# Weight placement, earlier transposes and two-bank gates in a float32r decoder kernel

## The chip, the cores and the metric

The kernel runs on one core of a Trainium2 chip. The metric is the time of one execution on the device in microseconds (us), the median of several runs. Five engines work side by side: PE (TensorE, the matmuls, with its weight loads shown as PEld), DVE (VectorE), ACT (ScalarE), POOL (GpSimd) and SP (SyncE), which here only issues DMA transfers.

## The reference

Two decoder layers over one sequence of 256 tokens, model width 2048, in float32. Cut to what matters here:

```python
# layer 0: recurrent block, then SwiGLU
y, xb = split(rms_norm(x) @ lru_w_in)            # 2048 -> 2 x 2048
xb = causal_conv4(xb)
r = sigmoid(block_diag(xb, w_rg)); i = sigmoid(block_diag(xb, w_ig))   # 8 blocks of 256
a = exp(-8 * r * softplus(-lam)); u = sqrt(1 - a*a) * (i * xb)
x += (scan(a, u) * gelu(y)) @ lru_w_out
x += (silu(g) * up) @ ffn_w_out   where g, up = split(rms_norm(x) @ ffn_w_in)   # width 5632
# layer 1: one shared K/V, sliding window attention with sinks, then SwiGLU again
k, v = split(rms_norm(x) @ w_kv);  x += attention(rms_norm(x) @ w_q, k, v) @ w_o
x += swiglu(x)
```

## The kernel before

All activations stay in SBUF with features on the partitions and the 256 tokens along the free dimension. A float32 product is made of three float32r matmuls: each operand is cut into a high part and a low part, and high times high, high times low and low times high are summed in PSUM.

**Jobs.** The whole program is a list of jobs, one for each weight chunk of 128 x 1024 floats (two tiles of 128 rows by 512 columns). `stream()` walks the list. At step i it issues the DMA of chunk i + 4 into one of four `raw` tiles, cuts chunk i + 3 into `hi` (copied by ACT, L368) and `lo` (the rest, by DVE, L369), and issues the matmuls of chunk i. Work on activations runs as background tasks, which are stepped between jobs by counters of the DVE and ACT time spent. A scheduler may still move instructions on an engine past each other. A normal chunk has 24 matmuls: 8 weight blocks of 128 x 128, each once against the high half and once against the low half of an activation slot (`a`, `b`), and 8 low weight blocks against the high half (`l`). In `group()` the activations `s` are the loaded weights' counterpart, the moving operand, and `hi`/`lo` are loaded into the array; in `fast_group()` it is the other way round.

**Stages.** Layer 0 begins with `lru()`: groups x0 to x3 and y0 to y3 (8 jobs each) and eight `gates` jobs g0 to g7 in the order `x0 x1 x2 g0 x3 g1 y0 g2 g3 y1 g4 g5 y2 g6 g7 y3`; then `project(lru_out)`. `ffn()` has 22 groups of 8 chunks and then `project(ffn_out)` (4 groups of 22 chunks): groups 0 to 3 are plain (L416), the even groups 4 to 20 are fast groups, the odd ones between are direct groups (L416). A fast group does seven of its eight chunks (`PAIRS`) with seven block products in place of eight, for which `mix()` makes sums of weight blocks in two more slots `mh` and `ml` (DVE and ACT, L380 to L385), and ends in `joined()`, which leaves a result that must be transposed on PE (L785, four transposes; `turn`). These transposes are put in `pend` and done later by `flush()`: in chunk 4 of the next fast group, or in chunk 6 of the last direct group. Layer 1 is `kv()`, `attn()` and again `ffn()`.

**Placement.** From `raw0` on, all tiles are multiples of 256 bytes, but for the 64-byte tile `step`, which stands between slot s6 and slot s7. So the near slots (s0 to s6) stand in phase with `hi` and `lo` (phase 0 of 256 bytes), and the far slots (s7 to s36) at phase 64. Activations stand in far slots. `parts()` sets where in its tile a chunk's `hi` and `lo` begin:

```python
o = 0 if self.jobs[i][2] is not None else self.STEP      # STEP = 32 floats = 128 bytes
```

So a normal chunk's weights stand at phase 128 and those of direct groups, of fast groups and of the queries at phase 0. Of the mixed chunks those in `EVEN` (chunks 0 and 4) put their sums in far slots (phase 64, the phase of the activations), the others in near slots. In the chunks in `EVEN` the products with the sums come first.

**Banks.** PSUM has eight banks of 512 floats. A normal group takes four, a gates job takes four and uses half of each, a fast group takes four. `free_bank` appends to the list of free banks, and `bank()` and `mbank()` take the first of it. `bank4()` takes a whole set of four if all of it is free.

## Time and profile before

| | |
|---|---|
| time before, median of 3 runs | 1972.53 us (1972.23 to 1976.43) |
| profiled execution, its own time | 1969.53 us |
| its span in the profile | 1967.4 us |
| PE busy | 1961.1 us, 16752 matmuls |
| PEld busy | 1933.4 us |
| DVE busy | 1523.4 us |
| ACT busy | 1128.6 us |
| granted TensorE clock | full in every stretch |

The page of the profile gives busy time by engine, the busy share in 40 slices, the chain that ended last, and the costliest groups of instructions with the mean duration of one and the idle time before them. Matmuls overlap: one lasts 277 ns in the records, but the next starts some 113 ns after it. So "PE busy 100%" tells only that PE never stood idle for long; the pace is read from how many matmuls start in a stretch. The windows view counts all instructions that touch a stretch, so its count is one or two above the number of starts. PEld starts are cleaner, since the load of a matmul stands some 0.11 us ahead of it.

### The profile page before, as it was taken

Reading aid. Unit: us, or ns where it says so; the run is one execution under the profiler, and the core shown is the slowest. Engines: PE = TensorE matmul, PEld = TensorE weight load, DVE = VectorE, ACT = ScalarE, POOL = GpSimd, SP = SyncE. Lnnn points to the kernel's source line nnn. Section 1 sums busy time; section 2 is a strip of 40 time slices with the busy share of each in tenths; the row PEclk is TensorE's granted clock in tenths of the full one; section 3 lists DMA queues with packets and bytes.
Section 4 is the critical chain, followed back from the end, with each engine's and each line's share of the span. In section 5 each row is a group of like instructions: output and inputs, shape, how many; then the busy total and the mean of one; then the engine's idle time right before and its main releaser. Section 6 shows DMA issues by size and latency. Waiting matters only on the chain.

```text
span 1967.4 us, 40634 instructions
## 1 busy us (share of the span) xinstructions
PE 1961.1 (100%) x16752; PEld 1933.4 (98%) x16752; DVE 1523.4 (77%) x2425; ACT 1128.6 (57%) x1620; POOL 0.2 (0%) x4
## 2 busy tenths in 40 slices
PE   9999999999999999999999999999999999999999
PEld 9999999999999999999998889999999999999999
DVE  7988868999999997544667777698999998954443
ACT  7798746555556565434556766565555555743332
POOL 0000000000000000000000000000000000000000
PEclk9999999999999999999999999999999999999999
DMA  8555665566655667555554335656556565666663
GB/s 282 182 187 182 221 216 193 187 201 212 209 199 193 206 203 245 184 186 189 185 181 158 121 129 178 212 192 204 202 195 205 194 216 198 233 207 204 204 204 128
DMA packets 107321, 384.98 MB, mean 196 GB/s; under 512 B 11904, under 2 KB 14080, under 8 KB 107136
## 3 DMA queue, kind: packets, MB, share of 16 engines
q1 hardware_dynamic: 106848, 381.99, 58.7%
q8 instruction: 131, 2.15, 0.4%
q10 hardware_dynamic: 288, 0.40, 0.1%
q14 instruction: 54, 0.44, 0.1%
HBM read 376.06 MB, written 6.29 MB: 194 GB/s over the span
## 4 chain that ended last, share of the span: by engine, by line
PE 97%; DVE 1%; ACT 1%; issue 0%; DVEq 0%; ACTq 0%
PE b L416 67%; PE b L595 18%; PE b L1316 5%; PE b L567 2%; PE b L1167 1%; DVE lo L369 1%; PE b L1231 1%; PE b L1212 1%; PE b L1122 1%; ACT s L134 0%; DVE s L147 0%; PE b L785 0%; ACT hi L368 0%; PE b L1290 0%; PE b L1356 0%
## 5 line engine op out<-in xcount | busy, mean ns | idle before, releaser
L416 PE MATMUL b<-s,hi 128*128 128x256 f32 x7936 | 1026.6, 277 | 1.3 <-ACT s L134 1.3
L416 PEld LDWEIGHTS b<-s,hi 128*128 128x128 f32 x7936 | 968.8, 188 | 2.7 <-ACT s L134 1.9
L369 DVE TENSOR_TENSOR lo<-raw,hi 128x1024 fp32r<-128x1024 f32 (+1 forms) x579 | 702.3, 1219 | 338.4 <-ACT hi L368 332.9
L368 ACT ACTIVATE hi<-raw 128x1024 fp32r<-128x1024 f32 (+1 forms) x579 | 608.4, 1056 | 491.5 <-PE b L416 435.9
L416 PE MATMUL b<-s,lo 128*128 128x256 f32 x3968 | 588.4, 277 | 0.0
L416 PEld LDWEIGHTS b<-s,lo 128*128 128x128 f32 x3968 | 514.3, 188 | 0.0
L383 ACT ACTIVATE s<-s 128x1024 fp32r<-128x1024 f32 x126 | 131.6, 1057 | 170.2 <-DVE s L382 170.2
L595 PE MATMUL b<-s,s 128*128 128x256 f32 x1512 | 195.9, 279 | 0.0
L595 PEld LDWEIGHTS b<-s,s 128*128 128x128 f32 x1512 | 183.0, 189 | 0.0
L595 PE MATMUL b<-hi,s 128*128 128x256 f32 x1044 | 178.0, 277 | 0.0
L385 DVE TENSOR_TENSOR s<-s,s 128x1024 fp32r<-128x1024 f32 x126 | 153.6, 1219 | 5.9 <-ACT s L383 5.9
L595 PEld LDWEIGHTS b<-hi,s 128*128 128x128 f32 x1044 | 152.3, 188 | 0.0
L595 PE MATMUL b<-lo,s 128*128 128x256 f32 x522 | 132.5, 276 | 0.0
L380 DVE TENSOR_TENSOR s<-raw 128x512 f32<-128x512 f32 x126 | 86.4, 686 | 41.5 <-DMA raw<-in_ffn_in 41.4
L384 DVE TENSOR_TENSOR lo<-raw,hi 128x768 fp32r<-128x768 f32 x126 | 118.4, 950 | 0.0
L134 ACT ACTIVATE s<-s 128x512 fp32r<-128x512 f32 (+3 forms) x177 | 87.2, 522 | 50.7 <-DVE s L143 34.5
L379 ACT ACTIVATE hi<-raw 128x768 fp32r<-128x768 f32 x126 | 103.0, 834 | 14.6 <-ACT s L383 7.1
L595 PEld LDWEIGHTS b<-lo,s 128*128 128x128 f32 x522 | 92.6, 188 | 0.0
L1316 PE MATMUL b<-hi,s 128*128 128x512 f32 x256 | 83.9, 408 | 0.0
L143 DVE TENSOR_TENSOR s<-s,s 128x512 fp32r<-128x512 f32 (+2 forms) x143 | 74.5, 552 | 2.2 <-ACT s L134 2.2
L134 ACT ACTIVATE s<-b 128x256 fp32r<-128x256 f32 (+4 forms) x134 | 58.6, 469 | 25.6 <-PE b L1290 5.7
L143 DVE TENSOR_TENSOR s<-b,s 128x512 f32<-128x512 f32 (+3 forms) x126 | 63.6, 531 | 3.8 <-ACT s L134 2.6
(115 smaller groups left out, 1171.5 us busy)
## 6 DMA issues: line engine op xcount, KB each, us to landing
raw<-in_ffn_in SPq DMA_DIRECT2D x352, 512.0 KB, 3.4
raw<-in_ffn_out SPq DMA_DIRECT2D x176, 512.0 KB, 3.7
raw<-in_lru_in SPq DMA_DIRECT2D x63, 512.0 KB, 4.2
raw<-in_lru_out SPq DMA_DIRECT2D x32, 512.0 KB, 4.3
raw<-in_w_q SPq DMA_DIRECT2D x32, 512.0 KB, 3.3
raw<-in_w_o SPq DMA_DIRECT2D x32, 512.0 KB, 3.4
raw<-in_gate SPq DMA_DIRECT2D x8, 512.0 KB, 4.2
away<-s SPq DMA_DIRECT2D x8, 512.0 KB, 4.0
```

The source lines that it names most:

```text
L134: self.nc.scalar.activation(out, in_, func, **kw)
L143: self.nc.vector.tensor_tensor(out, a, b, op)
L368: self.nc.scalar.activation(hi[:, q], raw[:, q], AF.Copy)
L369: self.nc.vector.tensor_tensor(lo[:, q], raw[:, q], hi[:, q].bitcast(F32), ALU.subtract)
L379: act(hi[:, q], raw[:, q], AF.Copy)
L380: tt(two(d[:, 0:2 * T]), two(raw[:, T:3 * T]), raw[:, 0:T].unsqueeze(1).to_broadcast([P, 2, T]), ALU.subtract)
L383: act(mh[:, :], d[:, :], AF.Copy)
L384: tt(lo[:, q], raw[:, q], hi[:, q].bitcast(F32), ALU.subtract)
L385: self.mark = tt(ml[:, :], d[:, :], mh[:, :].bitcast(F32), ALU.subtract)
L416: self.nc.tensor.matmul(ps[f][:, 0:T], w, x2[k][:, c0:c1], start=f not in begun, stop=last and all(q[1] != f for q in todo[n + 1:]))
L595: nc.tensor.matmul(st["ps"][b][:, h % 2 * T:(h % 2 + n) * T], x, w, start=b not in st["begun"], stop=True, skip_group_check=True)
L1316: nc.tensor.matmul(st[g][b][:, :], x, q, start=c + kt == 0 and x is xh and q is wh, stop=c == 7 and kt == 1 and q is wl)
```

## The change

Four things change.

- `STEP` and the numbers that chose a placement become pairs (offset of `hi`, offset of `lo`, and for mixed chunks a third number). `LEVEL_W` = (32, 16) is new: `hi` at phase 128 as before, `lo` at phase 64, the phase of the far slots. It is used for 20 chunks: chunk 1 in each group of `project` (4 of `lru_out`, 4 of `ffn_out` in each layer, the 2 of `w_o` that go through `group`), chunk 1 of the plain groups 1 and 3 of each `ffn`, and chunk 6 of the last direct group of each `ffn`, ahead of whose products the last `flush` stands.
- In the fast groups the flush moves from chunk 4 to chunk 0. Chunk 4 loses its order (sums first) and its far place: its sums go to near slots as those of chunks 1, 2, 5, 6 and 7 do. Chunk 0 keeps both. The near slots become nine (s0 to s8).
- A gates job takes two banks instead of four, two results to a bank, and frees them after its four sigmoids.
- The background task of a y group waits 4 half-steps instead of 6 before it begins.

```diff
-    STEP = 32
+    PLAIN_W, LEVEL_W, PLAIN_X, MIXED, MIXED_FAR = (32, 32), (32, 16), (0, 0), (0, 0, 1), (0, 0, 2)
+    LEVEL = (1,)
...
-    EVEN = (0, 4)
...
-    NEAR = 7
+    NEAR = 9
...
-        o = 0 if self.jobs[i][2] is not None else self.STEP
-        return (q[i % 4][:, o:o + 1024] for q in (self.hi, self.lo))
+        at = self.jobs[i][2]
+        return (q[i % 4][:, o:o + 1024] for q, o in zip((self.hi, self.lo), at))
...
-        near = self.jobs[i][2] == 1
+        near = self.jobs[i][2] is self.MIXED
...
-    def group(self, src, nk, xs, done, last=False, four=False, pre=None, base=0):
+    def group(self, src, nk, xs, done, last=False, four=False, pre=None, base=0, level=()):
...
-            self.jobs.append((src(c), mm, 0 if c < base else None))
+            self.jobs.append((src(c), mm, self.PLAIN_X if c < base else self.LEVEL_W if c in level else self.PLAIN_W))
...
-            self.group(lambda c, g=g: w[g, c], nk, xs, done, g == 3)
+            self.group(lambda c, g=g: w[g, c], nk, xs, done, g == 3, level=self.LEVEL)
...
-            if c in self.EVEN:
+            if c == 0:
                 todo = todo[3:] + todo[:3]
...
-                if c == self.EVEN[1]:
+                if c == 0:
                     self.flush()
...
-            self.jobs.append((src(c), mm, (c in self.PAIRS) + (c in self.EVEN)))
+            kind = self.PLAIN_X if c not in self.PAIRS else self.MIXED_FAR if c == 0 else self.MIXED
+            self.jobs.append((src(c), mm, kind))
...
-                self.group(src, ND, xs, start, g == self.PLAIN - 1, True)
+                self.group(src, ND, xs, start, g == self.PLAIN - 1, True, level=self.LEVEL if g % 2 else ())
...
-                self.group(src, ND, xn, direct, g == NH // 2 - 1, True, 6 if end else None, 6 if end else 8)
+                self.group(src, ND, xn, direct, g == NH // 2 - 1, True, 6 if end else None, 6 if end else 8, (6,))
...
-                ps = [self.bank() for _ in range(4)]
+                ps = [self.bank() for _ in range(2)]
+                cut = lambda j: ps[j // 2][:, j % 2 * T:j % 2 * T + T]
...
-                            nc.tensor.matmul(ps[j][:, 0:T], (hi if high else lo)[:, c:c + P], x2[kt][:, q:q + T],
-                                             start=kt == 0 and high > q, stop=kt == 1 and not high)
+                            nc.tensor.matmul(cut(j), (hi if high else lo)[:, c:c + P], x2[kt][:, q:q + T],
+                                             start=j % 2 + kt == 0 and high > q, stop=True, skip_group_check=True)
...
-                    self.a(o[:, 0:T], ps[j][:, 0:T], AF.Sigmoid, bias=par[:, col:col + 1])
-                    self.free_bank(ps[j])
+                    self.a(o[:, 0:T], cut(j), AF.Sigmoid, bias=par[:, col:col + 1])
                     v.append(o)
+                for p in ps:
+                    self.free_bank(p)
...
-                    yield 6
+                    yield 4
```

The built order shows it at three places. In all rows `b0` to `b7` are the PSUM banks, `s` followed by a number is a slot of SBUF (up to 6 near before, up to 8 near after), the number behind the underline only counts tiles, and the brackets name the engine that an instruction waits for.

The first place is PE at the end of gates job g3 and the start of group y1, before:

```order
L927 MATMUL b1_140<-s30_1123,hi3_79 128x256 x2
L927 MATMUL b1_140<-s30_1123,lo3_83 128x256
L416 MATMUL b5_144<-s7_183,hi0_76 128x256 [waits Activation_49]
L416 MATMUL b5_144<-s7_183,hi0_76 128x256
L416 MATMUL b6_145<-s7_183,hi0_76 128x256 [waits Activation_49]
L416 MATMUL b6_145<-s7_183,hi0_76 128x256
L416 MATMUL b7_146<-s7_183,hi0_76 128x256 [waits Activation_49]
```

and after:

```order
L929 MATMUL b1_140<-s32_1123,hi3_79 128x256 x2
L929 MATMUL b1_140<-s32_1123,lo3_83 128x256
L416 MATMUL b5_144<-s9_183,hi0_76 128x256 [waits DVE_49,Activation_49]
L416 MATMUL b5_144<-s9_183,hi0_76 128x256
L416 MATMUL b6_145<-s9_183,hi0_76 128x256 [waits DVE_49]
L416 MATMUL b6_145<-s9_183,hi0_76 128x256
L416 MATMUL b7_146<-s9_183,hi0_76 128x256 [waits DVE_49]
```

Before, y1 takes the banks of gates job g2 and waits for g2's sigmoids on ACT; after, it takes the banks of group y0, which DVE emptied two jobs earlier.

The second place is PE around the transposes in the second fast group of layer 0. Before they stand in chunk 4, between the products of plain chunk 3 and the products with the sums (far slots s10 and s11):

```order
L595 MATMUL b0_139<-hi3_79,s27_4098 128x256 x4
L595 MATMUL b0_139<-lo3_83,s27_4098 128x256 x2
L785 MATMUL b6_145<-con_62,s34_4476 128x128 x4
L595 MATMUL b3_142<-s10_5236,s20_4153 128x256 [waits Activation_49]
L595 MATMUL b3_142<-s10_5236,s20_4153 128x256
L595 MATMUL b3_142<-s11_5237,s20_4153 128x256 [waits DVE_49]
```

After, they stand right behind the direct group (L416), ahead of chunk 0, and wait for ACT:

```order
L416 MATMUL b7_146<-s34_4330,hi3_79 128x256 x2
L416 MATMUL b7_146<-s34_4330,lo3_83 128x256
L786 MATMUL b6_145<-con_62,s22_4476 128x128 [waits Activation_49]
L786 MATMUL b6_145<-con_62,s22_4476 128x128 x3
L595 MATMUL b3_142<-s10_5103,s27_3911 128x256 x2
L595 MATMUL b3_142<-s11_5104,s27_3911 128x256 [waits DVE_49]
```

The bank that they write, b6, was the direct group's until then; in chunk 4 it had been free for four jobs.

The third place is ACT behind the gates jobs g2 and g3, before (the sigmoids read b5 to b0 for g2, b2 to b1 for g3):

```order
L134 ACT_TABLE_LOAD
L134 ACTIVATE s6_1670<-b5_144,par_61 128x256
L134 ACTIVATE s6_1670<-b6_145,par_61 128x256
L134 ACTIVATE s18_1673<-b7_146,par_61 128x256
L134 ACTIVATE s18_1673<-b0_139,par_61 128x256
L368 ACTIVATE hi2_78<-raw2_74 128x1024
L134 ACTIVATE s25_1705<-b2_141,par_61 128x256
L134 ACTIVATE s25_1705<-b3_142,par_61 128x256
```

and after:

```order
L134 ACT_TABLE_LOAD
L134 ACTIVATE s8_1670<-b2_141,par_61 128x256 x2
L134 ACTIVATE s20_1673<-b3_142,par_61 128x256 x2
L368 ACTIVATE hi2_78<-raw2_74 128x1024
L134 ACTIVATE s27_1705<-b4_143,par_61 128x256 x2
L134 ACT_TABLE_LOAD
L134 ACTIVATE s8_1670<-s8_1670,cc_63 128x256
L134 ACT_TABLE_LOAD
L134 ACTIVATE s28_1708<-b1_140,par_61 128x256 x2
```

The exponentials of g2 now stand between the sigmoids of g3, and each change of function there loads a table: over the whole program ACT has 31 table loads after and 25 before.

More of the change, by code (lines that the diff above doesn't have):

```diff
@@ L361, in split @@
         hi, lo = self.parts(i)
-        if self.jobs[i][2]:
+        if len(self.jobs[i][2]) > 2:
             self.mix(i, raw, hi, lo)
@@ L571, in mm @@
                     self.residual(g, ps, gains, r, part=g)
-            self.jobs.append((w[g, c], mm, None))
+            self.jobs.append((w[g, c], mm, self.PLAIN_W))
         for q in (range(last - 1), range(last - 1, last + 1)):
@@ L941, in mm @@
                     both.clear()
-            self.jobs.append((self.d["gate"][n], mm, None))
+            self.jobs.append((self.d["gate"][n], mm, self.PLAIN_W))
         both = []
@@ L1137, in mm @@
                     done(ps)
-            self.jobs.append((w[c], mm, None))
+            self.jobs.append((w[c], mm, self.PLAIN_W))
     def attn(self, xs, r, gains, rn):
@@ L1324, in mm @@
                     self.spawn(finish(g, st[g]))
-            self.jobs.append((w[g, c], mm, 0))
+            self.jobs.append((w[g, c], mm, self.PLAIN_X))
         self.qst = {}
```

## The prediction

> **What bounds the kernel now.** I read the page first.
>
> ```profile
> span 1967.4 us, 40634 instructions
> PE 1961.1 (100%) x16752; PEld 1933.4 (98%) x16752; DVE 1523.4 (77%) x2425; ACT 1128.6 (57%) x1620; POOL 0.2 (0%) x4
> ...
> PE 97%; DVE 1%; ACT 1%; issue 0%; DVEq 0%; ACTq 0%
> ```
>
> PE carries 97% of the chain, so a nanosecond per matmul is worth 16.8 us, and work on other engines counts only where PE waits for it. The profiled execution took 1969.53 us, 2.1 us beside its span; the median of the runs is 1972.53, so 3.0 us above. My sums go against 1969.53.
>
> Second I compared two stretches with the same program, `ffn_out` of layer 0 and of layer 1, in the windows view of L416 (columns: stretch, its length, PE busy and count, PEld busy and count, clock, DMA).
>
> ```profile
> 757.44:1009.00 251.56, 251.56 (x2138) 251.53 (x2136) 1.00 0.57 189
> 1722.10:1964.20 242.10, 242.10 (x2138) 242.06 (x2136) 1.00 0.59 190
> ```
>
> Both hold 2136 weight loads at the full clock. The first paces at 251.56/2136 = 117.8 ns, the second at 113.3. PE has a slow and a quick beat for one and the same form (far activations at phase 64 against weights at phase 128), and it kept the slow one for 252 us. The timeline of PE shows where they part, at the last transposes of each layer:
>
> ```profile
> 754.18 0.60 PE L785 MATMUL b<-con,s 128*128 128x128 f32 x4
> 754.53 2.13 PE L416 MATMUL b<-s,hi 128*128 128x256 f32 x16
> 756.50 1.10 PE L416 MATMUL b<-s,lo 128*128 128x256 f32 x8
> ...
> 1718.94 0.60 PE L785 MATMUL b<-con,s 128*128 128x128 f32 x4
> 1719.30 2.08 PE L416 MATMUL b<-s,hi 128*128 128x256 f32 x16
> ```
>
> The sixteen products behind the transposes take 2.13 us in one layer and 2.08 in the other: the break throws PE into either beat, and it stays there. Clock and DMA (the last three columns of the windows) are the same, so neither explains it. That the median run is 3.0 us above the profiled one fits one more such stretch: the 26 chunks behind the first norm of a `ffn` would lose 26 x 24 x 4.5 ns = 2.8 us. That is an estimate.
>
> Third, the fast groups. The timeline of PE in the second one, chunk 0 and then chunk 4:
>
> ```profile
> 425.45 1.60 PE L595 MATMUL b<-s,s 128*128 128x256 f32 x12
> 426.89 0.40 PE L595 MATMUL b<-hi,s 128*128 128x256 f32 x2
> 427.13 0.28 PE L595 MATMUL b<-lo,s 128*128 128x256 f32 x1
> 427.25 0.39 PE L595 MATMUL b<-hi,s 128*128 128x256 f32 x2
> 427.48 0.28 PE L595 MATMUL b<-lo,s 128*128 128x256 f32 x1
> 427.59 0.39 PE L595 MATMUL b<-hi,s 128*128 128x256 f32 x2
> ...
> 435.42 0.60 PE L785 MATMUL b<-con,s 128*128 128x128 f32 x4
> 435.77 1.68 PE L595 MATMUL b<-s,s 128*128 128x256 f32 x12
> 437.29 0.40 PE L595 MATMUL b<-hi,s 128*128 128x256 f32 x2
> ```
>
> Twelve products with far sums (both operands at phase 64) start from 425.45 to 426.89: 120.0 ns each. The next three take 0.36 us (120), the three after them 0.34 (113). So equal phases cost 6.7 ns a product, and such a run ends in the quick beat, even right behind transposes (435.77).
>
> Fourth, the gates. Windows over all engines, each from a pair of gates jobs (g2 g3, g4 g5, g6 g7) to the end of the first chunk of the y group behind it (DVE and ACT are the third and fourth pair of columns):
>
> ```profile
> 122.69:131.72 9.03, 8.82 (x74) 8.42 (x73) 6.32 (x14) 8.45 (x15) 0.00 (x0) 1.00 0.50 176
> 150.78:161.27 10.49, 9.19 (x74) 8.62 (x73) 10.14 (x21) 7.23 (x15) 0.00 (x0) 1.00 0.54 184
> 180.31:189.95 9.64, 9.21 (x74) 8.64 (x73) 9.64 (x20) 6.79 (x14) 0.00 (x0) 1.00 0.58 196
> ```
>
> Each holds three jobs, 72 starts, and would take 72 x 113.3 ns = 8.16 us. The sum is 29.16, so 4.68 us are lost in waits for banks.
>
> **The change part by part.**
>
> *The slow beat.* In each `ffn_out` the chunk behind the last transposes, and one chunk in each group after it, becomes a level chunk: eight products at equal phases. By the rows at 425.45 and 435.77 that forces the quick beat. It takes away 251.56 - 242.10 = 9.5 us. Bounds: 0 (it does not force it) and 9.5. I take -9.5, since both far runs quoted, one behind transposes, end so.
>
> *Price of the level chunks.* 8 products x 6.7 ns and 0.02 us for the return are 0.074 us; 20 chunks make +1.5. Bounds 0.5 and 2.
>
> *Chunk 4 with near sums.* It loses 12 x 6.7 ns + 0.02 = 0.10 us in 18 fast groups: -1.8. Its sums are still made three chunks ahead; the two near slots more hold them, so no engine waits for room. That leaves two far slots less, which I cost at nothing: activations had 30, and a shortage would show as DVE or ACT work put off, covered by the same three chunks. The copy of the transposed result on ACT moves with the transposes, and a fetch of parked activations on SP moves a place ahead of one weight load (weights come four chunks ahead); both at nothing for the same reason. If that cover is gone, PE waits for `hi` or `lo`.
>
> A rule speaks against these three terms. The Trainium skill, "TensorE: Matmul & The Clock Gate", Part 2, step 4, says that TensorE reads SBUF through two independent ports, one for the moving operand and one for weight loads. By it placement would cost nothing and the three terms would be zero. The trace disagrees, 120.0 against 113.3 ns in rows that differ in placement alone.
>
> *Transposes at chunk 0.* At chunk 4 their bank had been free for long. Now it is the bank of the direct group that ends there, and the first weight load waits for ACT's Silu from it (the `h<-b` row). The three rows below show that Silu in a usual group, the product that the transposes will precede, and the latest Silu, at the boundary 467.23.
>
> ```profile
> 550.28 0.39 ACT L134 ACTIVATE h<-b 128x256 f32<-128x256 f32 x1 [0.82 <-PE b L416]
> 550.77 0.28 PE L595 MATMUL b<-s,s 128*128 128x256 f32 x1
> ...
> 467.23 1.60 PE L595 MATMUL b<-s,s 128*128 128x256 f32 x12
> 467.74 0.36 ACT L134 ACTIVATE h<-b 128x256 f32<-128x256 f32 x1
> ```
>
> Signal time comes from y1's start: a sigmoid from 127.95 (0.47 us) and the product that waited for it at 128.48, 0.06 us later.
>
> ```profile
> 127.95 0.47 ACT L134 ACTIVATE s<-b,par 128x256 f32<-128x256 f32 x1
> ...
> 128.48 0.38 PE L416 MATMUL b<-s,hi 128*128 128x256 f32 x1 [0.21 <-ACT s L134]
> ```
>
> At 550 the Silu ends at 550.67, the load could go at 550.73, and went at 550.66 (0.11 ahead of its product): 0.07 us late. At 467 it ends at 468.10: 1.04 us late. The same reading at the 16 boundaries that get a flush gives 0.07 at 11 of them and 0.27 to 1.04 at 5, behind a late `hi` copy: 0.8 us at the eleven and 2.7 at the five, +3.5. Bounds 1.1 (all usual) and 16.6 (all as the latest). I take the sum as it stands, since ACT's order up to that Silu is the same before and after. Behind the waiting load stands all of PE, since it issues in order; ACT and DVE work on meanwhile.
>
> *Gates in two banks.* y0's four and two each for g2 and g3 are eight, so nobody takes a bank just used, and the waits for sigmoids go: -4.7. Late next is ACT. The six table loads more fall behind the gates, each 1.28 us:
>
> ```profile
> L134 ACT ACT_TABLE_LOAD x23 | 29.5, 1283 | 0.4
> ```
>
> They are 7.7 us of work where ACT was busy for 22.5 of 29.2 us, with some idle around. Behind that stands DVE, which from y3's end until the last chunks of the first `lru_out` group, that need y3's results, hardly paused:
>
> ```profile
> 204.00:230.00 26.00, 26.00 (x232) 26.00 (x231) 25.56 (x49) 18.81 (x32) 0.00 (x0) 1.00 0.60 187
> ```
>
> If PE arrives earlier it may wait there; the earlier start of the y task (4 half-steps) helps. Bounds: -4.7 and +3.0 (all loads in the open, 7.7 - 4.7). I take -3.5, near the lower end, since weights are cut three chunks ahead, about 8 us, against 2.6 to 3.8 us of loads in each stretch.
>
> The Trainium skill, "ScalarE: Activation LUTs", What ACT_TABLE_LOAD costs, gives some 2.66 us for each switch, with a drain of 1.38. By that the six would be 16 us of ACT and this term positive. The row shows 1283 ns and 0.4 us idle ahead of all 23, so the trace does not bear the drain out.
>
> **Sum.** -9.5 + 1.5 - 1.8 + 3.5 - 3.5 = -9.8, so 1969.5 - 9.8 = 1959.7 us, 12.8 us or 0.65% under the median.
>
> **The rivals.**
>
> *Placement does not steer the beat.* PE falls back into the slow beat behind the level chunks, as it did behind transposes. Then -9.5 goes and 1959.7 + 9.5 = 1969.2 is left, 0.17% under the median. Against it: both far runs end quick.
>
> *ACT bound behind the gates.* The loads are in the open: +3.0 instead of -3.5, 1966.2. For it: ACT at 8.45 of 9.03 us in the first window.
>
> *The slow beat elsewhere.* The bank waits in the gates also broke the beat three times, and no level chunk stands before `lru_out`. If the first norm leaves the slow beat, 58 chunks x 24 x 4.5 ns = 6.3 us are lost: 1966.0. Against it: the 113.3 pace held behind this break in the profiled run.
>
> *Slower.* The transposes wait for ACT in every group. At the latest row's 1.04 us in all 16 that is 16.6 instead of 3.5, 1972.8, no change. It decides for slower than 1976.5 from (16.8 + 3.5)/16 = 1.27 us each, which no boundary shows; DVE, which holds ACT up there, would have to fall behind by more in every group.
>
> **How the numbers follow.** 0.2% of 1972.53 is 3.9 us, about what a measurement of this kernel can tell from no change; the bounds are 1968.6 and 1976.5. Forecast 0.62; ACT bound 0.12 and slow beat elsewhere 0.10, both faster; placement without effect 0.09, no change; long waits for ACT 0.07, of which 0.04 are slower. Faster 0.84, same 0.12, slower 0.04. The range: the low ends of the unknown prices (transposes 1.1, gates -4.7, level 0.5) give 1955.1, and I go to 1954; upward it takes in the two faster rivals with their spread, to 1968.
>
> **What would show it.** Right: 2136 loads in each `ffn_out` in about 243 us; 113 ns products in chunk 4 of the fast groups; three gates windows of about 8.2 us; a short wait of PE for ACT's `h<-b` at 16 transposes, about 0.1 us at most of them. Wrong: 117.8 ns behind a level chunk; PE waiting for ACT or DVE between 130 and 230 us; waits of 1 us at most transposes, or a slow beat in a stretch that was quick.

## The result and the profile after

The changed kernel takes 2007.28 us (median of 4 runs, 2003.44 to 2011.44) against 1972.38 for the kernel before on the same chip: ratio 1.0177, 95% interval 1.0156 to 1.0198. The forecast was 1959.7 us, in a range of 1954 to 1968. The profiled execution took 2011.44 us, 41.9 more than before's 1969.53; it is the slowest of the four, so the stages below add up to some 7 us more than the medians differ by. The page after:

```profile
span 2009.6 us, 40670 instructions
PE 1988.2 (99%) x16752; PEld 1958.8 (97%) x16752; DVE 1527.0 (76%) x2425; ACT 1135.1 (56%) x1626; POOL 0.2 (0%) x4
...
PE 89%; DVE 5%; ACT 3%; issue 2%; DMA 1%; ACTq 0%; DVEq 0%
```

PE's share of the chain fell from 97% to 89%, so PE now waits for others. But PE is also busy 27 us longer with the same 16752 matmuls, so the matmuls themselves became slower. Stage by stage, in us, from the start of a stage's first chunk to that of the next (the experiments, e1 to e13, come below; "fast" are the fast and direct groups of `ffn_in`, counted from behind the first twelve products of the first fast chunk, 1.4 us past its start; what lies between `ffn_out` 0 and `w_o` took 148.6 to 148.7 us in every column):

| stage | before | after | e1 | e2 | e3 | e4 | e7 | e8 | e10 | e12 |
|---|---|---|---|---|---|---|---|---|---|---|
| lru_in and gates | 201.5 | 202.2 | 205.9 | 203.1 | 201.7 | 202.3 | 201.5 | 201.5 | 203.5 | 200.9 |
| lru_out | 87.0 | 95.2 | 94.7 | 93.5 | 90.3 | 90.5 | 87.0 | 87.0 | 90.8 | 87.0 |
| ffn_in 0, plain | 89.5 | 91.9 | 89.5 | 91.9 | 91.9 | 92.9 | 89.5 | 89.5 | 89.5 | 89.5 |
| ffn_in 0, fast | 374.7 | 381.3 | 381.4 | 378.7 | 380.2 | 378.7 | 380.1 | 374.7 | 374.7 | 374.7 |
| ffn_out 0 | 248.7 | 248.8 | 239.4 | 248.8 | 248.8 | 248.7 | 239.4 | 239.6 | 248.7 | 239.6 |
| w_o | 103.1 | 104.7 | 103.1 | 104.5 | 104.7 | 103.1 | 103.1 | 103.1 | 103.1 | 103.0 |
| ffn_in 1, plain | 89.5 | 91.9 | 89.5 | 91.9 | 92.9 | 89.5 | 89.5 | 89.5 | 89.5 | 89.5 |
| ffn_in 1, fast | 374.5 | 385.5 | 378.4 | 378.7 | 377.6 | 378.7 | 382.8 | 374.5 | 374.5 | 374.5 |
| ffn_out 1 | 239.3 | 248.7 | 239.3 | 248.7 | 248.7 | 248.6 | 248.6 | 239.3 | 239.3 | 239.3 |

Three things are to be read from the first two columns. First, both `ffn_out` now pace slowly. The windows view of L416 (stretch, length, PE and PEld with counts, clock, DMA):

```profile
775.30:1026.86 251.56, 251.56 (x2138) 251.56 (x2136) 1.00 0.57 189
1754.82:2006.38 251.56, 251.56 (x2138) 251.56 (x2136) 1.00 0.56 183
```

251.56/2136 = 117.8 ns in both, at the full clock; the second had 242.10 before. The timeline of PE at the first level chunk of `ffn_in` 0, a place where before had 113.3 throughout, shows the moment. The same three pieces in before, a whole chunk and the start of the next:

```profile
321.57 1.98 PE L416 MATMUL b<-s,hi 128*128 128x256 f32 x16
323.39 1.07 PE L416 MATMUL b<-s,lo 128*128 128x256 f32 x8
324.29 1.98 PE L416 MATMUL b<-s,hi 128*128 128x256 f32 x16
```

and after:

```profile
330.42 1.98 PE L416 MATMUL b<-s,hi 128*128 128x256 f32 x16
332.23 1.12 PE L416 MATMUL b<-s,lo 128*128 128x256 f32 x8
333.19 2.05 PE L416 MATMUL b<-s,hi 128*128 128x256 f32 x16
335.07 1.10 PE L416 MATMUL b<-s,lo 128*128 128x256 f32 x8
```

The sixteen high products of the level chunk start from 330.42 to 332.23 (113.3 ns each), its eight low ones from 332.23 to 333.19 (120.0), and the sixteen of the next, normal chunk from 333.19 to 335.07: 117.8. PE enters the level chunk quick and leaves it slow. Behind every one of the 20 level chunks it paces 117.8, whether it came in quick or slow.

Second, PE waits at the transposes. In before it waited at none of them, and for 3.1 us in all elsewhere. The waits of PE after (us in total, times, longest):

```profile
PE b L786 <- ACT h L134: 10.9, 9, 2.4
PE b L416 <- ACT hi L368: 3.3, 3, 2.0
PE b L416 <- ACT s L134: 2.4, 1, 2.4
PE b L1359 <- DVE hi L1356: 1.3, 1, 1.3
PE b L416 <- DVE s L143: 0.5, 1, 0.5
```

Line 1 are the transposes; lines 2, 3 and 5 lie between 133 and 232 us, behind the gates and in the first chunks of `lru_out`. One of the long waits in the timeline of ACT and PE:

```profile
563.71 1.06 ACT L383 ACTIVATE s<-s 128x1024 fp32r<-128x1024 f32 x1 [2.35 <-DVE s L382]
564.68 0.83 ACT L379 ACTIVATE hi<-raw 128x768 fp32r<-128x768 f32 x1
565.41 0.36 ACT L134 ACTIVATE h<-b 128x256 f32<-128x256 f32 x1
...
565.83 0.66 PE L786 MATMUL b<-con,s 128*128 128x128 f32 x4 [2.40 <-ACT h L134]
566.24 2.48 PE L595 MATMUL b<-s,s 128*128 128x256 f32 x12
```

ACT comes to the Silu at 565.41 because it stood before that for DVE's sums (L382) and cut two parts of chunk 2 of the fast group first. PE waits 2.40 us, and the twelve far products behind the wait take 2.48 us instead of 1.60: from the fifth on they start 214 ns apart, at half the clock.

Third, the gates. Their own windows are what was forecast (8.16 us each, or near):

```profile
122.57:130.76 8.19, 8.19 (x74) 8.19 (x73) 5.48 (x13) 7.57 (x13) 0.00 (x0) 1.00 0.56 194
152.31:160.46 8.15, 8.15 (x75) 8.15 (x74) 8.04 (x17) 7.86 (x13) 0.00 (x0) 1.00 0.70 247
181.12:189.58 8.46, 8.46 (x75) 8.46 (x74) 8.43 (x20) 7.28 (x12) 0.00 (x0) 1.00 0.63 216
```

The third is in the slow beat (8.46/72 = 117.5 ns). The bank waits are gone, and the two stages together still take 8.9 us more.

### The profile page after: what moved, and what is told of

It reads as the page before. It is cut to its first block, busy times and chain, and to the rows that moved or that the text cites. A ratio compares the mean times of both kernels' runs of the same rounds, so it can differ in the third digit from the quotient of the medians.

```text
span 2009.6 us, 40670 instructions
## 1 busy us (share of the span) xinstructions
PE 1988.2 (99%) x16752; PEld 1958.8 (97%) x16752; DVE 1527.0 (76%) x2425; ACT 1135.1 (56%) x1626; POOL 0.2 (0%) x4
## 4 chain that ended last, share of the span: by engine, by line
PE 89%; DVE 5%; ACT 3%; issue 2%; DMA 1%; ACTq 0%; DVEq 0%
PE b L416 60%; PE b L595 17%; PE b L1319 4%; PE b L567 2%; DVE lo L369 2%; DMA raw<-in_ffn_in 1%; ACT s L134 1%; ACT hi L368 1%; ACT L134 1%; PE b L1170 1%; PE b L1234 1%; DVE s L147 1%; DVE s L143 1%; PE b L1215 1%; PE b L1125 1%
## 5 line engine op out<-in xcount | busy, mean ns | idle before, releaser
L416 PE MATMUL b<-s,hi 128*128 128x256 f32 x7936 | 1041.1, 279 | 6.2 <-ACT hi L368 3.3
L416 PEld LDWEIGHTS b<-s,hi 128*128 128x128 f32 x7936 | 982.0, 189 | 7.6 <-ACT hi L368 4.1
L416 PE MATMUL b<-s,lo 128*128 128x256 f32 x3968 | 596.4, 279 | 0.0
L416 PEld LDWEIGHTS b<-s,lo 128*128 128x128 f32 x3968 | 520.8, 189 | 0.0
L134 ACT ACTIVATE s<-s 128x512 fp32r<-128x512 f32 (+3 forms) x177 | 87.4, 522 | 61.2 <-DVE s L143 40.9
L379 ACT ACTIVATE hi<-raw 128x768 fp32r<-128x768 f32 x126 | 103.1, 834 | 14.6 <-PE b L595 4.1
L134 ACT ACTIVATE s<-b 128x256 fp32r<-128x256 f32 (+4 forms) x134 | 58.7, 470 | 24.8 <-PE b L1234 7.0
```

The source lines that it names most:

```text
L134: self.nc.scalar.activation(out, in_, func, **kw)
L379: act(hi[:, q], raw[:, q], AF.Copy)
L416: self.nc.tensor.matmul(ps[f][:, 0:T], w, x2[k][:, c0:c1], start=f not in begun, stop=last and all(q[1] != f for q in todo[n + 1:]))
```

## The experiments

In the expectations of e5 and e9 phases are given as byte addresses modulo 256; these lie 128 above the phases of the sections above. Offset 32 is phase 128 above and 0 there, offset 0 is phase 0 above and 128 there, far slots are 64 above and 192 there. Below I say offsets.

**e1, no level chunks.** The changed kernel with

```diff
-    LEVEL = (1,)
+    LEVEL = ()
...
-6 if end else 8, (6,))
+6 if end else 8)
```

> The changed kernel without level chunks (all 20 are plain again), the rest as changed. Theory A, the level chunks themselves throw PE into the 117.8 ns beat and leave it there: the stretches that paced at 117.8 behind a level chunk go back to 113.3, which by the stage times is 2.5 us in lru_out, 2.4 in each of the two plain parts of ffn_in, 1.6 in w_o and 9.4 in the second ffn_out, 18 us in all: about 1989 us against 2007. Rival B, the slow beat comes from the new waits of PE and the level chunks are innocent: 2005 to 2009 us and the same stretches slow.

1979.33 us, ratio to before 1.0046 (1.0026 to 1.0065): 28.0 us less than the changed kernel. The plain parts, `w_o` and `ffn_out` 1 are back at before's values (table). So theory A; and 28 instead of 18 in good part because `ffn_out` 0 came out quick as well (239.4), where the break at the last transposes happened to end quick and no level chunk threw it back. The rest of the profiled execution differs too, in both directions: PE paced 117.8 ns from its first chunk on to the end of `lru_out`, so `lru_in` is 3.7 us longer and `lru_out` only 0.5 shorter, and the second fast stretch is 7.1 shorter. In the stretches that theory A names, `lru_out` left out, and `ffn_out` 0 the profile gains 25.2 us.

**e2, transposes at chunk 4.** The changed kernel with

```diff
-                if c == 0:
+                if c == 4:
                     self.flush()
```

> The changed kernel with the transposes of a seven product group back at chunk 4 (level chunks, near sums in chunk 4 and gates as changed). Theory A, PE waits at chunk 0 for a Silu that ACT reaches late, and only because the transposes need that bank there: the two fast stretches go from 766.8 us back to before's 749.2 less 1.8 for the near sums, so about 1988 us. Rival B, the near sums with two far places less put DVE and ACT behind, and PE waits for them wherever the transposes stand: less than 5 us gained, 2002 us or more, with PE waiting for hi or lo in the seven product groups.

2001.47 us, 1.0157 (1.0135 to 1.0179): 5.8 us less, between what the two theories give. The waits for the Silu are gone, as theory A says, and PE waits in no fast group. But the fast stretches stay at 378.7 each, 4 us above before, with no wait in them: that is rival C of e4, told below.

**e3, gates in four banks.** The changed kernel with the gates as before:

```diff
-                ps = [self.bank() for _ in range(2)]
+                ps = [self.bank() for _ in range(4)]     # and ps[j][:, 0:T] for cut(j)
...
-                    yield 4
+                    yield 6
```

> The changed kernel with the gates in four banks and the y task 6 half-steps later, as before; level chunks and transposes as changed. Theory A, the new waits in the first 300 us come from the gates: lru_in goes from 202.2 back to 201.5 us and lru_out loses its waits and half clock products (5.6 of its 8.2 us more) but keeps 2.5 of slow beat: about 2001 us. Rival B, the waits in lru_out come from its level chunks: only 0.7 us gained, 2006.5 us.

1999.51 us, 1.0144 (1.0122 to 1.0166): 7.8 us less. In the profile the two stages of the gates give 5.4 us of it (0.5 and 4.9). `lru_out` keeps 3.3 us, with level chunks. Theory A. Which of the two edits of the gates part it is, e6 and e10 tell.

**e4, near sums alone.** The changed kernel with the edits of e1, e2 and e3 together. Against before, this is left:

```diff
-    EVEN = (0, 4)
-    NEAR = 7
+    NEAR = 9
...
-            if c in self.EVEN:
+            if c == 0:
                 todo = todo[3:] + todo[:3]
```

> The kernel before with one part of the change: chunk 4 of a seven product group keeps its weight sums in near places (9 instead of 7), the transposes stay at chunk 4. Theory A, the term of the sum: -1.8 us, 1970.6 us, and 113 ns products in chunk 4. Rival B, DVE and ACT fall behind for want of far places: slower than before by 1 us or more. Rival C, without a far run behind them the transposes at chunk 4 leave PE in the slow beat until the next far chunk at chunk 0: four chunks of 21 products in 16 groups at 4.5 ns, +6 us, 1978 us.

1988.3 us, 1.0092 (1.0067 to 1.0116): rival C, and more of it. No new wait of PE appears. Without a far run behind them the transposes leave PE slow in every second group, up to the far run of the next group's chunk 0 (4 us in each fast stretch, in e2 as well). In the profiled execution a bank wait in the gates left `lru_out` and the plain part of `ffn_in` 0 slow as well. And both `ffn_out` are slow; windows of L416:

```profile
768.60:1020.20 251.60, 251.60 (x2138) 251.51 (x2136) 1.00 0.58 189
1737.40:1989.00 251.60, 251.60 (x2138) 251.51 (x2136) 1.00 0.56 182
```

So the far run of chunk 4 was no 0.10 us of waste: it mends the beat behind the break.

**e5, a probe of places.** On e4's kernel single chunks of both `ffn_out` got other offsets, normal chunks (32, 32) between them:

```diff
+        for i, at in self.PLACES.items():   # 45 chunks: (16, 32), (16, 16), (0, 0), (16, 0), (32, 16), ...
+            self.jobs[i] = (*self.jobs[i][:2], at)
```

> A probe of the two beats, on the kernel with near sums in chunk 4 alone: in both ffn_out stages single plain chunks are put at other offsets (high part, low part), with plain chunks (32, 32) between them. Read is the pace of the chunks behind each. Theory A, the length of the run at equal phases picks the beat (8 products as in a level chunk leave PE in 117.8, 12 as in a far chunk in 113.3): behind (16, 32) and (16, 16), with 16 and 24 such products, the pace is 113.3. Theory B, the phases of the products behind the run pick it (far activations at phase 192 against weights at phase 0, where the far chunk is left with 128 against 192): 117.8 behind (16, 32) and (16, 16) as well, and another pace only where the run is left into other offsets. Theory C, any run of equal phases toggles or keeps the beat that was there: what follows depends on what stood before.

1986.0 us, one execution alone; it is read for its paces. Theory B. Timeline of PE: a normal chunk in the slow beat, a chunk at (0, 0), a normal one; then a (16, 0) chunk that was entered slow, and a normal one; then (16, 16), and a normal one:

```profile
868.74 2.05 PE L417 MATMUL b<-s,hi 128*128 128x256 f32 x16
870.62 1.11 PE L417 MATMUL b<-s,lo 128*128 128x256 f32 x8
871.57 2.05 PE L417 MATMUL b<-s,hi 128*128 128x256 f32 x16
873.46 1.10 PE L417 MATMUL b<-s,lo 128*128 128x256 f32 x8
874.39 1.98 PE L417 MATMUL b<-s,hi 128*128 128x256 f32 x16
...
1803.58 2.08 PE L417 MATMUL b<-s,hi 128*128 128x256 f32 x16
1805.50 1.07 PE L417 MATMUL b<-s,lo 128*128 128x256 f32 x8
1806.41 1.98 PE L417 MATMUL b<-s,hi 128*128 128x256 f32 x16
...
1876.76 2.08 PE L417 MATMUL b<-s,hi 128*128 128x256 f32 x16
1878.68 1.12 PE L417 MATMUL b<-s,lo 128*128 128x256 f32 x8
1879.64 2.05 PE L417 MATMUL b<-s,hi 128*128 128x256 f32 x16
```

Sixteen products in 2.05 are the slow beat, in 1.98 the quick one, in 2.08 equal phases. What all 45 chunks show:

| placed chunk | equal run, left into | entered | behind it |
|---|---|---|---|
| (32, 16), (16, 32), (16, 16), (0, 16) ahead of (32, 32) | 8 to 48 products, into offset 32 | quick or slow | slow, each time |
| (16, 0); (32, 16) ahead of (0, 0) | 16 or 8 products, into offset 0 | quick or slow | quick, each time |
| (0, 0) | none; back to offset 32 | slow, twice; quick, once | quick |
| (32, 0) | none | slow, three times | slow |
| (48, 48); (32, 48) | equal modulo 128 | quick, twice, and slow; slow, twice | quick and slow, as entered; slow once, quick once |

Behind a run at equal phases its length plays no part. What is decisive is which weights come behind it. And a whole chunk at offset 0 takes PE from slow to quick with no equal phases at all, though its low part alone there does not, and the last row fits no simple rule.

**e6, two banks alone.** The kernel before with one of the two edits to the gates:

```diff
-                ps = [self.bank() for _ in range(4)]
+                ps = [self.bank() for _ in range(2)]
+                cut = lambda j: ps[j // 2][:, j % 2 * T:j % 2 * T + T]
```

> The kernel before with one part of the change: the gates in two banks (the y task still 6 half-steps late, no level chunks, transposes and far runs as before). Theory A, the six more table loads make ACT the bound behind the gates: the bank waits go (4.7 us) and longer waits for hi and for a sigmoid take their place; the first 290 us are 3 to 6 us longer than before's 288.5, so 1975 to 1978 us. Rival B, the waits come from the y task that starts 4 instead of 6 half-steps late: with 6 the term of the sum holds, -3.5, 1969 us.

1970.45 us (1958.71 to 1976.55 in ten executions), 0.9997 (0.9980 to 1.0014). No wait of PE in the first 300 us, 25 table loads under L134 instead of 23. Neither theory is settled by the time: in the profiled execution PE had fallen into the slow beat at its first wait and paced 117.8 ns until the gates at 138 us. e12 takes this out.

**e7, earlier transposes alone.** The kernel before, far runs at chunks 0 and 4, with

```diff
-                if c == self.EVEN[1]:
+                if c == 0:
                     self.flush()
```

> The kernel before with one part of the change: the transposes at chunk 0 instead of chunk 4; the far runs at chunks 0 and 4 stay, with 7 near places. Theory A, the moved transposes alone make ACT's Silu late: PE waits some 10 us in all for it, and the two fast stretches take 758 to 765 us instead of 749.2: 1980 to 1988 us. Rival B, the Silu is as late as in before's rows, +3.5 us, 1976 us, and only together with the near sums it is later.

1972.93 us, 1.0013 (1.0000 to 1.0026). The median is 3.5 us above before's 1969.46, which is the term of rival B, but its ten executions scatter from 1968.96 to 1982.66. The profiled one is the slowest of them, and theory A holds in it: the fast stretches take 762.9 instead of 749.2, with this line among the waits of PE:

```profile
PE b L785 <- ACT h L134: 9.2, 12, 2.3
```

The median is 9.7 us under that execution. In it the first `ffn_out` was quick and the second slow; an execution with both quick would be 9.4 us shorter, which would fit, but no other execution has a profile. So the waits are shown, and what they cost in the median is not. The profiles of the changed kernel, e1 and e3, which have the transposes at chunk 0 too, show 10.9, 9.5 and 7.3 us of the same wait.

**e8, shifted chunks.** The kernel before, chunk 1 of each plain group from `lru_out` on at offset 0 (22 chunks; the expectation miscounts them as 16):

```diff
+    SHIFTED = (1,)
...
-            self.jobs.append((src(c), mm, 0 if c < base else None))
+            self.jobs.append((src(c), mm, 0 if c < base or c in shifted else None))
```

> The kernel before with its second chunk of each plain group (16 chunks) put at offset 0 instead of 32, nothing else: no run at equal phases at all. Theory B, the beat is set by the phase of the weights that PE leaves a stretch with, and going from offset 0 back to 32 leaves it quick (the probe: slow to quick twice, quick to quick once): the first ffn_out drops from 248.7 to about 239.5 us and stays quick, so does any other slow stretch, about 1960 us in nearly every run, with less scatter than before's 1969 to 1976. Rival A, the pace of the probe came from the runs at equal phases around it: the shifted chunks change nothing, 1969 us.

1960.32 us (1959.86 to 1961.03), 0.9938 (0.9924 to 0.9953). Theory B. The windows of both `ffn_out`:

```profile
757.40:999.81 242.41, 242.41 (x2138) 242.37 (x2136) 1.00 0.60 196
1712.90:1955.00 242.10, 242.10 (x2138) 242.03 (x2136) 1.00 0.59 190
```

The first still enters slow behind the transposes and is quick from its third chunk on. The other shifted chunks were entered quick and left quick, in this profile. The four executions lie within 1.2 us, where before's scatter by 7; that speaks for the beat as what made before's runs differ.

**e9, level chunks left into offset 0.** The changed kernel with one pair changed:

```diff
-LEVEL_W = (32, 16)
+LEVEL_W = (16, 0)
```

> The changed kernel with one pair of numbers changed: a level chunk has its high part at 16 and its low part at 0, instead of 32 and 16. It has sixteen products at equal phases instead of eight, and leaves them into weights at phase 128 instead of 0. Theory B, the exit picks the beat: all stretches behind level chunks are quick, the time is that without level chunks (1979) plus 20 x (16 x 6.7 ns + 0.02 us) = 2.5, less the slow stretches that were left there in the first 300 us: 1977 to 1982 us. Rival A, a run at equal phases itself leaves PE slow: 2007 us as in the changed kernel.

1979.84 us, 1.0040 (1.0027 to 1.0054). Theory B: twice the products at equal phases, 27 us less than the changed kernel, and within 0.5 us of e1, which has none. This rests on the time alone, since no profile shows its paces at the usual speed.

**e10, the whole gates part.** e6 with

```diff
-                    yield 6
+                    yield 4
```

> The kernel before with the whole gates part of the change: two banks, and the y task 4 half-steps late. Against the run with two banks alone (1970.5 us, 25 table loads on ACT, no wait of PE there). Theory A, the earlier y task puts its functions between the sigmoids of the gates: 29 table loads, PE waits for ACT's hi and for a sigmoid again, the first 290 us are 5 to 9 us longer: 1975 to 1979 us. Rival B, the start of the y task makes no difference by itself, and the waits of the changed kernel came from its nine near places: 1970 us.

1976.3 us, 1.0024 (1.0014 to 1.0034): theory A. ACT has 29 table loads under L134, and the waits of the changed kernel are there without the two more near places and without level chunks (waits of PE from 100 to 300 us):

```profile
PE b L416 <- ACT hi L368: 2.9, 3, 2.0
PE b L416 <- ACT s L134: 1.7, 1, 1.7
PE b L416 <- DVE s L143: 0.5, 1, 0.5
```

**e11, near sums in chunk 0.** e8 with chunk 0 of the fast groups near instead of far:

```diff
-    EVEN = (0, 4)
+    EVEN = (4,)
```

> The kernel before with the shifted chunks and with near sums in chunk 0 instead of far ones (chunk 4, behind the transposes, keeps its far run; 7 near places). The far run at chunk 0 has no break ahead of it to mend, so it should go for nothing: 18 x 0.10 = 1.8 us less than the shifted chunks alone, 1958 us. Rival, chunk 0 needs it (the direct group ahead ends in the slow beat, or the near places make DVE late): 1960 us or more.

1964.18 us, 0.9958 (0.9941 to 0.9974), 3.9 more than e8: the rival. PE comes quick out of the direct group and goes 117.8 in chunk 0 at once, until chunk 4. So the far run at chunk 0 mends a break too, that of the changed operands.

**e12, shifted chunks and two banks.** e8 with the shift in `lru_in` as well and the gates of e6:

```diff
-            self.group(lambda c: w[g, c], ND, xs, done, g == 3)
+            self.group(lambda c: w[g, c], ND, xs, done, g == 3, shifted=self.SHIFTED)    # x groups likewise
```

> The kernel with the shifted chunks (also in the groups of lru_in) and the gates in two banks, the y task 6 half-steps late. Theory A, two banks alone do bring what the prediction said, about 4 us of the 4.7 lost in bank waits, and the run with two banks alone hid it behind 45 chunks at 117.8 ns (45 x 24 x 4.5 ns = 4.9 us): 1960.3 - 4 = 1956 us. Rival B, ACT's two more table loads and what stands behind them take it back: 1960 us.

1959.24 us (1959.07 to 1960.34), 0.9940 (0.9925 to 0.9954). That is 1.1 us under e8 and not the 4 of theory A, and by the two ratios (0.9940 and 0.9938) no gain at all. The bank waits are gone and one new wait stands at 137.77:

```profile
PE b L417 <- ACT hi L369: 2.0, 1, 2.0
```

It costs 2.0 us and half clock behind it. So rival B in good part. In e6 PE came later, in the slow beat, and did not wait there; that this gave ACT the time is the likely reason.

**e13, transposes at chunk 2.** e8 with

```diff
-                if c == self.EVEN[1]:
+                if c == 2:
                     self.flush()
```

> The kernel with the shifted chunks and the transposes at chunk 2 of a seven product group; far runs at chunks 0 and 4, 7 near places. Theory A, what cost time at chunk 0 was the bank whose Silu ACT had not reached: at chunk 2 it is done, PE waits for no Silu, and only the break's beat is left, at most 2 chunks of 24 x 4.5 ns in 16 groups until the far run at chunk 4 mends it, 3.5 us: 1960 to 1964 us. Rival B, transposes ahead of chunk 4 put DVE's order out and leave PE waiting for hi or lo or the Silu all the same: 1966 us or more.

1968.91 us, 0.9989 (0.9976 to 1.0003), 8.6 more than e8. The Silu is out of the waits, as theory A says, but others have come, as rival B says:

```profile
PE b L596 <- DVE lo L385: 1.3, 3, 0.6
...
PE b L596 <- DVE s L386: 0.3, 1, 0.3
```

They are 1.6 of the 7.4 us that the fast stretches lost in its profile; much of the rest is slow beat (three direct groups paced 117.7 ns or more).

## Why the prediction was wrong, point by point

**The slow beat (-9.5): the wrong sign, and the largest error.** Level chunks cost 28.0 us (e1), of the 34.9 by which the kernel became slower, and gain nothing. The reading that far runs end quick was right, and is right in the runs here. The step that failed is the conclusion from them: "By the rows at 425.45 and 435.77 that forces the quick beat." Those runs are left into products whose weights are far activations, with `hi` and `lo` moving; a level chunk is left into `hi` weights at offset 32, with far activations moving. I took equal phases for the cause, and e5 and e9 show that it is what follows: 8, 16, 24 or 48 products at equal phases end slow into offset 32, 8 or 16 end quick into offset 0. The trace of before had only runs of one exit among its far chunks, so two rows that agreed were one case seen twice. What the prediction set against its own reading, that placement would cost nothing, is not borne out either: e8 moves 22 chunks by 128 bytes and takes 0.62% off. It had concluded that from the two independent read ports of which the Trainium skill tells ("TensorE: Matmul & The Clock Gate", Part 2, step 4). No run here shows the ports themselves. The rival "placement does not steer the beat" had the symptom, PE slow behind level chunks, and the wrong cause; it also priced only what would stay slow, not the quick stretches that a level chunk would slow down.

**Price of the level chunks (+1.5).** Right in size: the eight products at 332.23 took 120.0 ns each.

**Chunk 4 with near sums (-1.8).** In the changed kernel the term holds: an undisturbed pair of groups takes 41.71 us (the second row below) against 41.80. But alone it costs 16 us in the median (e4). 8 of them stand in the fast stretches, where the far run had mended the beat behind the transposes; most of the rest is slow beat in other stretches. The two parts of the change needed each other, which the sum did not say.

```profile
560.55:606.37 45.82, 43.42 (x369) 43.23 (x368) 41.08 (x57) 24.76 (x30) 0.00 (x0) 0.96 0.61 196
606.37:648.08 41.71, 41.71 (x370) 41.71 (x369) 37.77 (x53) 23.84 (x28) 0.00 (x0) 1.00 0.61 201
```

**Transposes at chunk 0 (+3.5, bounds 1.1 and 16.6).** The mechanism was right, the size was not: the two fast stretches took 766.8 instead of 749.2, so in this execution the term is 17.6 + 1.8 = 19.4 us. 10.9 are waits for the Silu; by the starts of the products half clock behind the three waits of over 2 us adds some 4 (the first row above: 45.82 instead of 41.71, of which 2.4 is the wait), and the slow beat behind one of them 1.5. The step that failed is "ACT's order up to that Silu is the same before and after". The order at the Silu was; the lead was not. DVE and ACT run ahead of PE by what `raw`, `hi` and `lo` hold. In the direct group ahead of the longest wait of layer 0, DVE stood 3.2 us before it cut the fourth chunk; in before it made the four cuts of the same group in one go (timeline of DVE, before and then after):

```profile
525.22 4.83 DVE L369 TENSOR_TENSOR lo<-raw,hi 128x1024 fp32r<-128x1024 f32 x4
```

```profile
544.77 1.23 DVE L369 TENSOR_TENSOR lo<-raw,hi 128x1024 fp32r<-128x1024 f32 x1 [3.21 <-ACT hi L368]
```

DVE was busy for 37.8 of 41.7 us (the second row above), so it makes such a pause good only slowly. The pause at that cut is not new: it was 0 to 1.1 us in the sixteen groups before and 0.3 to 3.2 after, and one wait of 2.4 us in layer 1 has a pause of only 1.0 ahead of it. What PE feels is the lead that is left. It can be measured: from the end of DVE's last cut of a chunk to that chunk's first product. At the last chunk of the eight direct groups ahead of a fast group in layer 0 it was as follows, and so was the gap of PE ahead of the transposes (from the start of the last product to theirs, less the usual 0.115; this is a little more than the idle time in the rows):

| direct group at, us (after) | 414.9 | 456.6 | 499.4 | 541.5 | 587.3 | 629.0 | 670.7 | 712.8 |
|---|---|---|---|---|---|---|---|---|
| lead before, us | 4.8 | 4.1 | 4.9 | 6.0 | 5.9 | 6.0 | 6.0 | 5.5 |
| lead after, us | 5.7 | 3.9 | 4.7 | 2.5 | 5.5 | 5.3 | 4.6 | 3.9 |
| gap ahead of the transposes, us | 0 | 1.1 | 0.4 | 2.6 | 0 | 0 | 0.4 | 1.2 |

Each wait follows the lead: none at 5.3 and more, 0.4 at 4.6 and 4.7, 1.1 to 1.2 at 3.9, 2.6 at 2.5; and the long wait gives the lead back. The eight groups of layer 1 go the same way: no gap at 5.2 and more, 0.2 at 4.9, 0.7 at 4.4, 1.1 at 4.0, and 2.4 and 2.6 at 2.6 and 2.5. I had counted with the leads of before. The cap of 16.6 was the latest row of a trace in which no lead fell under 4.1. e13 shows that the bank is only a part of it: at chunk 2, with the Silu long done, the move still costs 8.6 us, and in the profile 1.6 of them are waits for DVE and much of the rest is slow beat. What exactly shifts DVE's work there is not shown.

**Gates in two banks (-3.5, bounds -4.7 and +3.0).** The part as changed costs 7.8 us by the medians and 5.4 by the stages (e3), or 4.7 alone (e10). Its mechanism is the rival "ACT bound behind the gates", which had the chance of 0.12. Two steps failed. The six table loads were put down to the banks; the banks bring two (25 in e6) and the earlier y task, which I had counted as a help, the other four (29 in e10). And "weights are cut three chunks ahead, about 8 us, against 2.6 to 3.8 us of loads" does not hold at y1, where ACT goes back and forth between functions (timeline of ACT after):

```profile
130.27 0.85 ACT L134 ACTIVATE s<-b,par 128x256 f32<-128x256 f32 x2
131.14 1.28 ACT L134 ACT_TABLE_LOAD   x1
132.44 0.51 ACT L134 ACTIVATE s<-s,cc 128x256 f32<-128x256 f32 x1
132.97 1.28 ACT L134 ACT_TABLE_LOAD   x1
134.26 0.84 ACT L134 ACTIVATE s<-b,par 128x256 f32<-128x256 f32 x2
134.99 0.51 ACT L134 ACTIVATE s<-s,cc 128x256 f32<-128x256 f32 x1
135.52 1.28 ACT L134 ACT_TABLE_LOAD   x1
```

A function has come between two pairs of sigmoids, so three loads stand here where before has one (at 131.95, behind both pairs), and `hi` of the chunk that PE needs stands behind them. These are the two loads that the banks bring: e12, with the y task where it was, has the same three from 130.59 on, and the same wait. The drain of 1.38 us that the Trainium skill gives for each switch ("ScalarE: Activation LUTs", What ACT_TABLE_LOAD costs) is not seen here either: the function ahead of the load at 132.97 ends at 132.44 + 0.51 = 132.95, and behind it 132.97 + 1.28 is 134.25, and the sigmoid starts at 134.26.

**Range and chances.** The rivals at 117.8 ns behind a level chunk, at waits behind the gates and at waits of over 1 us at the transposes all came true at once, and each was larger than priced. The bound for slower, 1.27 us at every boundary, was not reached (10.9/16 = 0.7 in waits, 19.4/16 = 1.2 with what follows them); the kernel became slower than that bound's 1976.5 us by the level chunks above all, though e1, without them, is still 2.8 us over it.

## What to carry to other kernels

In this kernel a stream of matmuls held one of two paces for hundreds of microseconds, and what set it was the last break and the addresses behind it; so look for the stretch where one form paces in two ways, and try the place of single chunks before anything larger. A mechanism read from rows that are all of one kind is one observation: ask what else those rows share before it is moved to operands in other roles. When engines run close to full, a step moved to an earlier place must be costed by the lead of the engines that feed it over a whole period, not by how late they were when nothing depended on it.

## What the runs showed of the hardware that was not expected

One float32r product of 256 columns, at the full clock and without a wait, starts 113.3, 117.8 or 120.0 ns after the one before, by the byte addresses of the moving operand and the next weights modulo 256. 120.0 holds while the two are equal; 113.3 and 117.8 both go on at the same addresses until a wait, a transpose or a change of addresses. Products whose two addresses are equal modulo 128 only, (48, 48) in e5, fit none of the three: they start 113 to 124 ns apart, 118 to 119 on the mean. A whole chunk placed 128 bytes lower left PE quick behind it every time here (three in e5, 22 in e8), but only two of the three and one of the 22 were entered slow. Why the addresses matter is not shown.

PE's clock can fall to half after a wait of some 2 us: 2.4 us in the rows at 565.83 and 230.33 (here the twelve products take 2.48 us, where 1.52 is usual). In the profiles of the changed kernel, e1 to e4, e6 to e8 and e10 to e13 it did so after all five waits of 2.26 us and more, after three of the nine from 1.66 to 2.19 us (in e1, e10 and e12), and after none of 1.43 us or less. So the length of the wait alone does not decide it: 1.68 us, with 0.5 more a few products later, was enough in e1 and not in e10, and 2.19 us in e3 was not. In seven of the eight cases 15 or 16 starts in a row come 213 to 218 ns after the one before, some 3.3 us, until the pace is back.

```profile
230.33 0.86 PE L416 MATMUL b<-s,hi 128*128 128x256 f32 x5 [2.37 <-ACT s L134]
231.69 2.48 PE L416 MATMUL b<-s,hi 128*128 128x256 f32 x12 [0.50 <-DVE s L143]
```
